# Block 1 of a two-block transformer kernel: the last down-projection on all 512 tokens at once

## The chip, the cores and the metric

The kernel runs on one core of a Trainium2 chip, as one program from the loading of the inputs to the storing of the result. The metric is the time of one execution in microseconds (us) on the device; of several runs the median counts. The engines are named as the profile names them: PE is TensorE (matrix products; PEld is its loading of weights, which runs beside them), DVE is VectorE, ACT is ScalarE, POOL is GpSimd, and SP is SyncE, which issues most of the loads.

## The reference

One sequence of 512 tokens of width 1024 passes through two blocks of two layers each, in float32. The part that the change touches is the second half of a layer of block 1:

```python
for l in range(DEPTH):                                   # DEPTH = 2
    ...                                                  # three mixers, added to x
    u = _rms_norm(x, mlp_norm_g[l]) @ w_up[l]            # 1024 -> 4096
    x = x + jnp.square(jax.nn.relu(u)) @ w_down[l]       # 4096 -> 1024

    gate = jax.nn.sigmoid((_rms_norm(x, ple_norm_g[l]) @ w_ple_gate[l]).astype(jnp.float32))
    e = _rms_norm(p[l] @ w_ple_proj[l], ple_post_norm_g[l]).astype(jnp.float32)
    x = x + (gate * e).astype(x.dtype)
```

Here `_rms_norm` divides each token by the root of its mean square and multiplies by a gain, and `p[l]` is a second input of width 256. Block 2 has attention mixers and a gated feed-forward part with a convolution, each behind a modulated norm, and a last norm.

## The kernel before, in words

**Layout.** `x` is held transposed: eight tiles `x[m]` of 128 features by 512 tokens. A product in float32 is made of three matrix products of rounded parts: `mm3` (line 171) issues, for each 128 rows of the contraction, high by high (L176), low weight or high weight by the other's low part (L177, L178), all into one bank of the accumulator memory. `split` (line 134) makes the parts: ACT casts to the high part (L136), DVE subtracts (L137). `feat_group` (line 181) makes `ng` output tiles of 128 features for the tokens of each slice in `parts`; a slice is all 512 tokens (`FULL`) or one of two halves of 256 (`HALVES`).

**Banks.** An output tile goes to a bank by rotation (`mm`, line 105). Inside `wide` and `held` the rotation is over three names: `ps_mm` with 3 buffers, `ps_S` with 2 and `ps_T` with 2. A group can begin when the reader of the bank's last content is done. The small products of the norms take `ps_mm` too.

**Norms.** `norm_stats` (line 244) works on one half of the tokens in three steps. First the squares of the eight tiles are made on ACT (L252, L255) and added on DVE (L256, into `n_acc`). Then PE sums over the features with four small matmuls of one column (L260); DVE scales the sums (L121); POOL makes the inverse root in ten small operations (L122 to L128); ACT writes it on the diagonal of `n_dg`, twice (L264). Last, PE spreads it over the partitions (L267) and ACT copies the result to a tile `R` (L268). Below, a *chain* is the way from L260 to L267 of one half. The steps are a generator: `start` runs the first and queues the rest, and `tick` takes the next step when enough matmul work has been issued (table `PAUSES`, line 29).

**The end of a layer of block 1** is `mlp1` (line 900). The 4096 hidden features come in 8 chunks: `up(c)` makes 512 of them, `down(c)` multiplies them by their part of `w_down` and adds them into `yacc` (L947, DVE). `down(7)` adds its product straight to `x` (L942, DVE). Behind it six chains run one after the other while PE does other products:

- #1 and #2, for the halves 0 and 1: the norm of `x` ahead of the gate (`pre`, the result in `g_R`); beside its squares `hsplit` makes the parts of `x` times gain (ACT L283, DVE L284) that the gate's product reads;
- #3 and #4: the norm of `p @ w_ple_proj` (`enorm`). The product has 16 groups (L992 to L995, ACT copies them to `yacc`). Behind the norm, DVE multiplies the eight tiles of the half by gain and norm (L984, eight times);
- #5 and #6: the norm for the next layer or block (`nxt`), started behind each half of the gate.

The gate has eight groups for each half (weights `w_pg1`). Its sink `gsink` (lines 986 to 991) multiplies by `g_R` straight out of the bank (L988, DVE), takes tanh (L989, ACT), multiplies with `yacc` (L990, DVE) and adds to `x` (L991, DVE). L990 needs the result of L984.

**Order.** The program text says what depends on what; the order of the instructions on each engine is set when the program is built, by a scheduler that sees the whole program. On the chip each engine then takes its instructions strictly in that order. So a small edit can move instructions far from its place.

Of the kernel before, what the change touches and what calls it, by code (L numbers as in the profile page):

```python
# [39 lines left out]
FULL = (slice(0, S),)  # L40
HALVES = (slice(0, S // 2), slice(S // 2, S))
# [20 lines left out]
class Builder:  # L62
# [837 lines left out]
    def mlp1(self, l, fp, act, nxt):  # L900
# [4 lines left out]
        acts = {}  # L905
# [33 lines left out]
        def down(c):  # L939
            def sink(m, pt, sl):  # L940
                if c == 7:
                    nc.vector.tensor_tensor(self.x[m][:, sl], self.x[m][:, sl], pt, ALU.add)  # L942
                    return
                if c == 0:
                    nc.scalar.copy(yacc[m], pt)
                else:
                    nc.vector.tensor_tensor(yacc[m], yacc[m], pt, ALU.add)  # L947
                if c == 6:
                    nc.vector.tensor_tensor(yacc[m], yacc[m], R2, ALU.mult)
                    nc.vector.tensor_tensor(self.x[m], self.x[m], yacc[m], ALU.add)  # L950
            ws = [self.wload("w_dn1", l * 16 + c * 2 + g, 4 * 512) for g in range(2)]
            for sl in HALVES if c == 7 else FULL:
                for g in range(2):
                    self.feat_group(ws[g], 4, 4, acts[c], sink, 4 * g, (sl,))
                if c == 7:
                    self.start(pre(sl))
        up(0)
        self.flush()
# [2 lines left out]
        for c in range(1, 8):  # L961
            up(c)
            self.mod_part(l, fp, (c - 1) * 6, c * 6)
            down(c - 1)
# [7 lines left out]
        self.mod_part(l, fp, 42, 48)  # L972
        self.mod_done(l, fp)
        down(7)

        act, ee = pre.st["act"], yacc
# [19 lines left out]
        ws = [self.wload("w_pg1", l * 4 + g, 8 * 256, (lambda: self.mtile(fp)) if g >= 2 else None) for g in range(4)]  # L996
# [574 lines left out]
```

## Time and profile before

| | |
|---|---|
| runs | 2770.52, 2776.11, 2781.68 us; median 2776.11 |
| profiled execution | 2770.02 us; span of the trace 2768.2 us; mean granted clock of TensorE 0.989 |
| PE busy | 2691.5 us (97% of the span), 16360 matmuls |
| DVE, ACT, POOL busy | 1782.7 (64%), 1182.1 (43%), 233.0 us (8%) |
| `down(7)` on PE | layer 0 from 625.42 us, layer 1 from 1327.50 us |
| DMA | 285.59 MB, mean 103 GB/s |

The times in the trace are from the start of the span. A matmul's own duration overlaps the next one's, so the pace of PE is read from the distance between starts. The number in brackets at the end of a row of the timeline is the time that the engine sat idle before this instruction, and what ended it.

### The profile page before, as it was taken

Reading aid. Unit: us, or ns where it says so; the run is one execution under the profiler, and the core shown is the slowest. Engines: PE = TensorE matmul, PEld = TensorE weight load, DVE = VectorE, ACT = ScalarE, POOL = GpSimd, SP = SyncE. Lnnn points to the kernel's source line nnn. Section 1 sums busy time; section 2 is a strip of 40 time slices with the busy share of each in tenths; the row PEclk is TensorE's granted clock in tenths of the full one; section 3 lists DMA queues with packets and bytes.
Section 4 is the critical chain, followed back from the end, with each engine's and each line's share of the span. In section 5 each row is a group of like instructions: output and inputs, shape, how many; then the busy total and the mean of one; then the engine's idle time right before and its main releaser. Section 6 shows DMA issues by size and latency. Waiting matters only on the chain.

```text
span 2768.2 us, 42721 instructions
## 1 busy us (share of the span) xinstructions
PE 2691.5 (97%) x16360; PEld 2287.3 (83%) x16360; DVE 1782.7 (64%) x3888; ACT 1182.1 (43%) x2340; POOL 233.0 (8%) x606
## 2 busy tenths in 40 slices
PE   8999999999999999999999999999999999999998
PEld 7876988889977788778988777888889787888887
DVE  7677777568767767765863676655554476664555
ACT  4644532326374543233543555333234455532332
POOL 2000100002200010000122300000001310000000
PEclk9999999999999999999999999999999999999999
DMA  4211487332321127843323211233332312133222
GB/s 155 77 40 54 143 266 229 111 103 92 92 73 47 55 89 238 254 156 100 107 67 110 62 57 63 84 88 101 99 94 80 118 37 78 51 103 99 88 86 78
DMA packets 87644, 285.59 MB, mean 103 GB/s; under 512 B 10972, under 2 KB 15132, under 8 KB 87440
## 3 DMA queue, kind: packets, MB, share of 16 engines
q1 hardware_dynamic: 81280, 266.49, 30.1%
q0 software_dynamic: 5872, 16.35, 2.3%
q8 instruction: 128, 2.10, 0.3%
q14 instruction: 76, 0.62, 0.1%
q10 hardware_dynamic: 288, 0.03, 0.0%
HBM read 280.69 MB, written 2.14 MB: 102 GB/s over the span
## 4 chain that ended last, share of the span: by engine, by line
PE 80%; DVE 8%; DMA 5%; ACT 3%; issue 2%; POOL 2%; SPq 0%; DVEq 0%; ACTq 0%; POOLq 0%
PE ps_mm L176 13%; PE ps_mm L177 12%; PE ps_mm L178 12%; PE ps_T L176 5%; PE ps_T L177 5%; PE ps_T L178 5%; PE ps_S L176 5%; PE ps_S L177 5%; PE ps_S L178 5%; DMA wm<-w_mod 4%; PE ps_S L1091 2%; PE ps_o L1137 1%; DVE wm L1034 1%; PE ps_T L1131 1%; PE ps_S L582 1%
## 5 line engine op out<-in xcount | busy, mean ns | idle before, releaser
L136 ACT CAST wh<-wr 128x1024 fp32r<-128x1024 f32 (+4 forms) x414 | 406.6, 986 | 659.4 <-PE ps_mm L177 209.4
L137 DVE TENSOR_TENSOR wl<-wr,wh 128x1024 fp32r<-128x1024 f32 (+4 forms) x414 | 474.8, 1148 | 306.7 <-ACT wh L136 300.2
L176 PE MATMUL ps_mm<-slotA,wh 128*128 128x512 f32 (+1 forms) x632 | 227.1, 365 | 1.8 <-ACT slotA L317 0.7
L177 PE MATMUL ps_mm<-slotA,wh 128*128 128x512 f32 (+1 forms) x632 | 225.7, 359 | 2.0 <-DVE slotA L318 2.0
L178 PE MATMUL ps_mm<-slotA,wl 128*128 128x512 f32 (+1 forms) x632 | 224.7, 357 | 0.0
L176 PE MATMUL ps_mm<-wh,slotA 128*128 128x256 f32 (+3 forms) x688 | 207.6, 303 | 1.1 <-ACT slotB L1084 1.1
L178 PE MATMUL ps_mm<-wh,slotA 128*128 128x256 f32 (+3 forms) x688 | 205.9, 299 | 0.0
L177 PE MATMUL ps_mm<-wl,slotA 128*128 128x256 f32 (+3 forms) x688 | 205.9, 300 | 0.0
L1034 DVE CUSTOM_DVE_ANT_0 wm<-wm,sc 128x1024 f32<-128x1024 f32 x96 | 117.5, 1224 | 67.6 <-DMA wm<-w_mod 66.7
L136 ACT CAST m_h<-tmp 128x512 fp32r<-128x512 f32 (+1 forms) x122 | 71.3, 587 | 208.1 <-DVE tmp L913 171.8
L176 PE MATMUL ps_mm<-slotB,wh 128*128 128x512 f32 (+1 forms) x408 | 143.8, 357 | 3.4 <-ACT slotB L136 2.6
L176 PEld LDWEIGHTS ps_mm<-wh,slotA 128*128 128x128 f32 x688 | 131.1, 191 | 14.3 <-issue 10.6
L177 PE MATMUL ps_mm<-slotB,wh 128*128 128x512 f32 (+1 forms) x408 | 141.9, 349 | 0.0
L178 PE MATMUL ps_mm<-slotB,wl 128*128 128x512 f32 (+1 forms) x408 | 140.9, 346 | 0.0
L176 PEld LDWEIGHTS ps_mm<-slotA,wh 128*128 128x128 f32 x632 | 120.5, 193 | 21.3 <-issue 3.2
L177 PEld LDWEIGHTS ps_mm<-wl,slotA 128*128 128x128 f32 x688 | 131.1, 191 | 7.9 <-issue 6.8
L177 PEld LDWEIGHTS ps_mm<-slotA,wh 128*128 128x128 f32 x632 | 120.7, 191 | 19.8 <-DVE slotA L318 2.9
L178 PEld LDWEIGHTS ps_mm<-slotA,wl 128*128 128x128 f32 x632 | 120.8, 191 | 19.3 <-issue 3.9
L178 PEld LDWEIGHTS ps_mm<-wh,slotA 128*128 128x128 f32 x688 | 131.3, 191 | 4.5 <-issue 3.2
L1107 ACT ACTIVATE at_s<-at_s,at_st 128x512 f32<-128x512 f32 (+3 forms) x160 | 89.4, 559 | 104.0 <-DVE at_st L1105 96.2
L176 PE MATMUL ps_S<-m_h,wh 128*128 128x512 f32 (+1 forms) x355 | 129.4, 365 | 0.7 <-DVE yacc L947 0.4
L178 PE MATMUL ps_S<-m_h,wl 128*128 128x512 f32 (+1 forms) x355 | 129.2, 364 | 0.0
(633 smaller groups left out, 7183.9 us busy)
## 6 DMA issues: line engine op xcount, KB each, us to landing
wr<-w_up SPq DMA_DIRECT2D x152, 512.0 KB, 3.9
wm<-w_mod SPq DMA_DIRECT2D x96, 512.0 KB, 4.6
wr<-w_dn SPq DMA_DIRECT2D x64, 512.0 KB, 3.9
wr<-w_dn SPq DMA_DIRECT2D x32, 384.0 KB, 3.1
wr<-w_dn SPq DMA_DIRECT2D x32, 320.0 KB, 2.8
wr<-w_f SPq DMA_DIRECT2D x16, 512.0 KB, 3.7
wr<-w_pg SPq DMA_DIRECT2D x16, 512.0 KB, 3.8
wr<-w_t SPq DMA_DIRECT2D x12, 512.0 KB, 4.7
```

Source lines behind the costliest of these rows:

```text
L136: nc.scalar.copy(hi, src)
L137: nc.vector.tensor_tensor(lo, src, hi.bitcast(F32), ALU.subtract)
L176: nc.tensor.matmul(out, ah, bh, start=i == 0, stop=False)
L177: nc.tensor.matmul(out, ah, bl, start=False, stop=False)
L178: m = nc.tensor.matmul(out, al, bh, start=False, stop=i == n - 1)
L582: nc.tensor.matmul(pt, qs[f][b:b + 64, tt], qs[4][b:b + 64, k0:k0 + w], start=True, stop=True)
L1034: nc.vector.tensor_tensor_reduce(w, w, self.sc, 1.0, 0.0, ALU.mult, ALU.add, accum_out=self.mod[l][:, j:j + 1])
L1091: i = nc.tensor.matmul(pts[u], q, k, start=True, stop=True, tile_position=None if row is None else (row, 0))
L1107: nc.scalar.activation(s, s, AF.Exp, bias=st[:, 0:1], scale=-1.0, accum_out=st[:, 1:2])
L1131: nc.tensor.transpose(tp[:, c * P:c * P + P], s[:, c * P:c * P + P], self.ident)
L1137: nc.tensor.matmul(po[u * 64:u * 64 + 64], v(c, u), pT[:, c * P:c * P + P], start=c == 0, stop=c == t, tile_position=(0, u * 64))
```

## The change

The two groups of `down(7)` (four output tiles each) are no longer made once for each half of the tokens, but once for all 512. The norms of both halves are started behind them. The weights, the sums and the results are the same; `down(0)` to `down(6)` are as they were. Both layers of block 1 are touched.

```diff
             ws = [self.wload("w_dn1", l * 16 + c * 2 + g, 4 * 512) for g in range(2)]
-            for sl in HALVES if c == 7 else FULL:
-                for g in range(2):
-                    self.feat_group(ws[g], 4, 4, acts[c], sink, 4 * g, (sl,))
-                if c == 7:
+            for g in range(2):
+                self.feat_group(ws[g], 4, 4, acts[c], sink, 4 * g)
+            if c == 7:
+                for sl in HALVES:
                     self.start(pre(sl))
```

In each layer 192 matmuls of 256 columns become 96 of 512, and 16 additions of 128x256 become 8 of 128x512. The groups of `down(7)` fall from 16 to 8, so that every later group gets another bank of the rotation. The new order of the instructions has these places.

DVE in `down(7)` of layer 0, difference of the two orders (L942 adds a product to `x`, L284 and L256 are of chain #1, L137 is the low part of weights):

```order
-L942 TENSOR_TENSOR x<-x,ps_T 128x256
-L942 TENSOR_TENSOR x<-x,ps_mm 128x256
+L942 TENSOR_TENSOR x<-x,ps_T 128x512
 L950 TENSOR_TENSOR x<-x,yacc 128x512
-L942 TENSOR_TENSOR x<-x,ps_S 128x256
 L284 SCALAR_TENSOR_TENSOR slotA<-x,vec_0_89,slotA 128x256
-L256 TENSOR_TENSOR n_acc<-tmp,n_acc 128x256
-L942 TENSOR_TENSOR x<-x,ps_T 128x256
+L942 TENSOR_TENSOR x<-x,ps_mm 128x512
 L284 SCALAR_TENSOR_TENSOR slotA<-x,vec_0_89,slotA 128x256
```

A full-width addition now frees both halves of a tile at once, and the parts and squares of both halves come mixed behind it.

PE in layer 0 at L267 of chain #4 (`ps_mm_...`, `ps_S_...` are banks with the number of the tile that is in them; `slotA` and `m_h` are the parts of `x` and of gate weights). First the order of before:

```order
L178 MATMUL ps_S_7035<-slotA_6036,m_l_6492 128x256
L267 MATMUL ps_mm_6824<-n_dg_6821,ones_83 128x256 [waits Activation_49]
L176 MATMUL ps_mm_6890<-slotA_6022,wh_6467 128x256
L177 MATMUL ps_mm_6890<-slotA_6023,wh_6467 128x256
L178 MATMUL ps_mm_6890<-slotA_6022,wl_6468 128x256
```

Then that of the change:

```order
L178 MATMUL ps_T_6923<-slotA_6036,m_l_6380 128x256
L267 MATMUL ps_mm_6712<-n_dg_6709,ones_83 128x256 [waits Activation_49]
L176 MATMUL ps_S_6983<-slotA_6022,m_h_6397 128x256 [waits DVE_49]
L177 MATMUL ps_S_6983<-slotA_6023,m_h_6397 128x256
L178 MATMUL ps_S_6983<-slotA_6022,m_l_6398 128x256
```

Behind L267 stood a group into a `ps_mm` bank that waits for nothing, and the next group into a `ps_S` bank whose last reader comes behind L984 began 50 matmuls later; now such a group follows at once, and it waits for DVE. DVE's order at the same place has the reader (L988 of `ps_S_6778`, whose bank `ps_S_6983` takes) behind the eight L984, which need this L267:

```order
L984 SCALAR_TENSOR_TENSOR yacc_3377<-yacc_3377,vec1_0_89,R1_85 128x256
L284 SCALAR_TENSOR_TENSOR slotB_6734<-x_72,vec1_1_91,slotB_6733 128x256
L284 SCALAR_TENSOR_TENSOR slotB_6736<-x_72,vec1_1_91,slotB_6735 128x256
L256 TENSOR_TENSOR n_acc_6755<-tmp_6763,n_acc_6755 128x256
L284 SCALAR_TENSOR_TENSOR slotB_6738<-x_72,vec1_1_91,slotB_6737 128x256
L256 TENSOR_TENSOR n_acc_6755<-tmp_6766,n_acc_6755 128x256
L256 TENSOR_TENSOR n_acc_6755<-tmp_6769,n_acc_6755 128x256
L988 TENSOR_TENSOR tmp_6803<-ps_S_6778,g_R_3378 128x256
```

In before, two L988, out of `ps_mm_6890` and `ps_S_6920`, stood right behind the last L984.

PE in layer 1 at L267 of chain #3, in the order of the change:

```order
L177 MATMUL ps_T_13495<-slotB_12766,wh_13088 128x256
L267 MATMUL ps_mm_13272<-n_dg_13219,ones_83 128x256 [waits Activation_49]
L260 MATMUL ps_mm_13358<-ones_83,n_acc_13063 128x1 [waits DVE_49]
L260 MATMUL ps_mm_13358<-ones_83,n_acc_13063 128x1
L176 MATMUL ps_mm_13385<-slotB_12755,m_h_13130 128x256 [waits DVE_49]
```

L260 of chain #4 follows L267 of chain #3 without a product between; in before 25 matmuls stood there. The matmuls between L260 and L267 of each chain, counted from the two orders:

| chain | #1 | #2 | #3 | #4 | #5 | #6 |
|---|---|---|---|---|---|---|
| layer 0 before | 67 | 72 | 70 | 72 | 70 | 48 |
| layer 0 changed | 60 | 63 | 62 | 73 | 64 | 69 |
| layer 1 before | 67 | 72 | 71 | 80 | 68 | 72 |
| layer 1 changed | 66 | 59 | 65 | 31 | 25 | 72 |

Two chains in the middle of the layers of block 2 change as well: from 24 to 64 matmuls in its first layer, and from 47 to 14 in its second.

## Rows read from the trace of the kernel before

**Rows 1.** The page: its head and the busy time of each engine.
```profile
span 2768.2 us, 42721 instructions
PE 2691.5 (97%) x16360; PEld 2287.3 (83%) x16360; DVE 1782.7 (64%) x3888; ACT 1182.1 (43%) x2340; POOL 233.0 (8%) x606
```

**Rows 2.** Timeline, PE around the start of down(7): start, duration, instruction.
```profile
617.26 0.39 PE L176 MATMUL ps_T<-m_h,wh 128*128 128x512 f32 x1
...
619.98 0.39 PE L176 MATMUL ps_mm<-m_h,wh 128*128 128x512 f32 x1
...
625.42 0.28 PE L176 MATMUL ps_T<-m_h,wh 128*128 128x256 f32 x1
...
626.85 0.28 PE L176 MATMUL ps_mm<-m_h,wh 128*128 128x256 f32 x1
```

**Rows 3.** Groups of DVE from 600 to 650 us: count, then busy us, mean ns.
```profile
L950 DVE TENSOR_TENSOR x<-x,yacc 128x512 f32<-128x512 f32 x8 | 5.5, 687 | 0.1
...
L942 DVE TENSOR_TENSOR x<-x,ps_T 128x256 f32<-128x256 f32 x5 | 2.1, 419 | 0.6 <-PE ps_T L178 0.6
```

**Rows 4.** Timeline, PE and ACT in layer 0: chains #4, #5 and #6.
```profile
695.36 0.59 PE L267 MATMUL ps_mm<-n_dg,ones 128*128 128x256 f32 x2
...
696.25 0.35 ACT L268 COPY R<-ps_mm 128x256 f32<-128x256 f32 x1
...
698.90 0.50 PE L260 MATMUL ps_mm<-ones,n_acc 128*128 128x1 f32 x4
...
701.98 0.28 PE L176 MATMUL ps_S<-slotA,m_h 128*128 128x256 f32 x1
...
709.91 0.70 PE L267 MATMUL ps_mm<-n_dg,ones 128*128 128x256 f32 x2 [2.01 <-ACT n_dg L264]
...
727.71 0.51 PE L260 MATMUL ps_mm<-ones,n_acc 128*128 128x1 f32 x4
...
734.93 0.70 PE L267 MATMUL ps_mm<-n_dg,ones 128*128 128x256 f32 x2 [0.86 <-ACT n_dg L264]
```

**Rows 5.** Timeline, DVE in layer 0 around L984 behind chain #4.
```profile
692.27 0.47 DVE L284 SCALAR_TENSOR_TENSOR slotB<-x,vec,slotB 128x256 fp32r<-128x256 f32 x1
692.67 0.94 DVE L256 TENSOR_TENSOR n_acc<-tmp,n_acc 128x256 f32<-128x256 f32 x2
...
697.86 3.25 DVE L984 SCALAR_TENSOR_TENSOR yacc<-yacc,vec,R 128x256 f32<-128x256 f32 x8
701.03 0.42 DVE L988 TENSOR_TENSOR tmp<-ps_mm,g_R 128x256 f32<-128x256 f32 x1
701.36 0.42 DVE L988 TENSOR_TENSOR tmp<-ps_S,g_R 128x256 f32<-128x256 f32 x1
```

**Rows 6.** Timeline, DVE in layer 1: neighbours whose starts give three prices.
```profile
1398.64 0.42 DVE L256 TENSOR_TENSOR n_acc<-tmp,n_acc 128x256 f32<-128x256 f32 x1
1398.98 0.42 DVE L988 TENSOR_TENSOR tmp<-ps_mm,g_R 128x256 f32<-128x256 f32 x1
...
1399.64 1.22 DVE L137 TENSOR_TENSOR wl<-wr,wh 128x1024 fp32r<-128x1024 f32 x1
1400.78 0.42 DVE L988 TENSOR_TENSOR tmp<-ps_T,g_R 128x256 f32<-128x256 f32 x1
```

**Rows 7.** Timeline, PE in layer 1: chains #4 and #5, and L260 of #6.
```profile
1382.34 0.50 PE L260 MATMUL ps_mm<-ones,n_acc 128*128 128x1 f32 x4
...
1392.38 0.59 PE L267 MATMUL ps_mm<-n_dg,ones 128*128 128x256 f32 x2
...
1409.70 0.70 PE L267 MATMUL ps_mm<-n_dg,ones 128*128 128x256 f32 x2
...
1425.86 0.71 PE L260 MATMUL ps_mm<-ones,n_acc 128*128 128x1 f32 x4 [4.73 <-DVE n_acc L256]
...
1427.00 0.41 PE L178 MATMUL ps_mm<-slotA,wl 128*128 128x256 f32 x1
...
1429.56 0.32 PE L178 MATMUL ps_mm<-slotA,wl 128*128 128x256 f32 x1
```

**Rows 8.** Busy us of the engines in a stretch; PEclk is the granted clock.
```profile
1420.00:1430.00 10.00, 5.27 (x32) 5.07 (x31) 6.14 (x23) 3.89 (x12) 3.83 (x14) 0.83 0.16 38
```

**Rows 9.** Timeline, block 2: a chain of its first and one of its second layer.
```profile
1736.10 0.70 PE L267 MATMUL ps_mm<-n_dg,ones 128*128 128x256 f32 x2 [1.85 <-ACT n_dg L264]
...
2398.01 0.51 PE L260 MATMUL ps_mm<-ones,n_acc 128*128 128x1 f32 x4
2402.55 0.70 ACT L264 ACTIVATE n_dg<-ident,rt 128x128 f32<-128x128 f32 x2 [3.67 <-POOL rt L128]
```

## The prediction

> **What bounds the kernel now.** I read the head of the page first: PE is busy for 2691.5 of 2768.2 us [rows 1]. It is the engine that sets the end, and only about 77 us are left in which it is not busy. So an edit can gain in two ways, fewer or cheaper matmuls or one of the few idle stretches gone, and it can lose by making PE wait where it does not wait now. The second view is the timeline of PE at `down(7)`. A group of 12 matmuls of 512 columns takes 2.72 us (617.26 to 619.98), one of 256 columns 1.43 (625.42 to 626.85): 0.227 and 0.119 us for each, so that two halves cost a little more than one whole [rows 2]. The third view is the timeline of the six norm chains behind it. There I looked for a bracket behind L267, which says that PE came to it before the chain was done. In layer 0 only #5 (2.01 us) and #6 (0.86) have one [rows 4]; in layer 1 no L267 of block 1's six has one, but L260 of #6 is preceded by 4.73 us in which PE waits for DVE's sums [rows 7]. So the chains are nearly covered by products, and with little to spare. A chain's own length shows where PE waited for it: 727.71 to 734.93 is 7.2 us, 698.90 to 709.91 is 11.0 [rows 4]. The least in the trace is in block 2, from 2398.01 to the end of L264 at 2403.25, 5.2 us [rows 9]. Cover is read as matmuls between L260 and L267 times 0.12 us, plus 0.4 for L260 itself: 80 matmuls give 10.0, and the trace has 1382.34 to 1392.38 [rows 7].
>
> **The change, part by part.** All sums are against the profiled execution of 2770.0 us, which lies 6.1 below the median of the three runs, 2776.1.
>
> *Removed work.* In each layer 192 x 0.1195 = 22.95 us of matmuls become 96 x 0.2267 = 21.76: 1.2 us less, 2.4 in all, straight off PE. DVE's additions fall from 32 of 0.42 us to 16 of 0.69 [rows 3], 2.4 us less over both layers. That is worth nothing by itself, as PE is the cover; with PE waiting for DVE it would shorten a wait by at most that.
>
> [...]
>
> *Moved work.* The first half of `x` was complete after half of `down(7)`, and chain #1 then ran beside the second half. Now both halves are complete at its end: relative to the products behind it, chain #1 starts some 96 matmuls later, 11 us. The chains must run one after the other (one `n_dg`, one `R`), so that the series starts late and has to catch up. The table of matmuls between L260 and L267 shows where the order catches up: chains #1 to #3 lose 1 to 13 matmuls each, and in layer 1 #4 is left with 31 and #5 with 25. POOL's ten operations for each chain keep their order, and no wait is added there. On SP a few loads of weights change places; no product in these stretches waited for a weight, and I cost that at nothing, because the same loads stand ahead of the same groups.
>
> *Chain #2.* Covered by 63 matmuls in layer 0 (8.0 us) and 59 in layer 1 (7.5). The length with an idle DVE is 7.2. But L121 now stands behind casts and sums: in layer 1 two L137 of 1.14 us [rows 6] are right ahead of it. With 1.2 and 1.6 us for that the waits are **0.4 and 1.3 us**. Bounds: nothing (length 5.2), and 3.0 and 3.5 (11.0). I take values near 7.2, since this is the same stage.
>
> *Layer 0, behind chain #4.* 73 matmuls (9.2 us) cover it. But right behind L267 stands a group into a `ps_S` bank. Its last reader is an L988 that DVE reaches only after the eight L984, which need this L267. In before that place held a `ps_mm` group, and a `ps_S` group with such a reader came 50 matmuls later, at 701.98, when L988 (701.36 + 0.42) had just left the bank [rows 4, 5]: no more than 0.2 us to spare. Now the cover is gone. From L267 to that L988 it was 6.0 us; six operations, three L284 (0.40) and three L256 (0.34), now stand where one L988 (0.33) stood [rows 5, 6], 1.9 more. 7.9 and 0.4 for L988 make 8.3 from L267, less 0.2 for L267 itself: 8.1 us. That is the upper bound; the lower is 6.9, since 1.2 of it was DVE still busy (R was there at 696.60, L984 began at 697.86). I take **7.5**. What is queued behind: L260 of #5 and everything that follows on PE.
>
> [...]
>
> [...]
>
> *Layer 0, #5 and #6.* #5 now starts after the wait, on a quieter DVE, with 64 matmuls (8.1) and #6 has 69 (8.7) in place of 48, against a length of 7.2. Both brackets go: **-2.0 and -0.9**. Layer 0: -1.2 + 0.4 + 7.5 + 1.4 - 2.9 = **+5.2**.
>
> *Layer 1.* #4: 31 matmuls cover 4.1 us of a chain of 5.2 to 7.2: between 1.1 and 3.1, I take **2.5**, nearer the length in this stage. Then a `ps_T` group waits as in layer 0, but 96 matmuls (11.5 us, and 0.6 for the two L260 and L267) after L267. DVE needs, from L267, about 3.2 until it is through with its backlog (2.5 in layer 0 [rows 4, 5], and the two halves' L984 now follow closer), 3.5 for L984 and one L990, eleven short operations of 0.34, three L137 of 1.14 and L988: 14.2 us. **2.1**; bounds 0 and 3. #5: 25 matmuls cover 3.4 us; 7.2 less 3.4 is 3.8, and L121 stands behind fourteen short operations, of which little sticks out: **4.0**, bounds 1.8 and 7.6. From there on DVE sets the pace: L267 of #5 to L260 of #6 took 16.2 us with PE idle 4.73 at its end [rows 7], the same operations stand there now, so what is late at L267 is late at L260. [...] Layer 1: -1.2 + 1.3 + 2.5 + 2.1 + 4.0 = **+8.7**.
>
> *Block 2.* The wait of 1.85 [rows 9] goes, as 64 matmuls cover it. In the other layer 14 matmuls (2.1 us) stand against 5.2: 3.1 new. **+1.2**; bounds -2 and +3.
>
> Sum: 5.2 + 8.7 + 1.2 = 15.1. 2770.0 becomes 2785.1, and on the median of the runs 2776.1 becomes **2791 us**, 0.54% slower. A measurement of this kernel tells about 0.5%, 14 us, from no change; the forecast lies at that edge.
>
> **Rivals.**
> *1. The norms stay covered: not slower.* Place: L267 of #4 and #5 in layer 1, and the `ps_S` bank in layer 0. If DVE, ACT and POOL, which wait beside PE, ran the chains in less than the cover, only the savings would be left: 2.4 of matmuls and the brackets of 2.0, 0.9 and 1.85, 7.2 us, 2769. It decides at a chain of 3.4 us or less. Against it: no chain in the trace is under 5.2. For it: these lengths are read from stretches in which DVE was busy, and in layer 1 of before no L267 waited. Chance 0.10, with 0.03 beyond 0.5% faster.
> *2. The late start is given back in the tail of layer 1.* While PE waits in layer 1, DVE can go on with sinks and casts that stand later now. If they fill the waits, the 16.2 us after #5 shrink, by no more than the 4.73 that PE idled there and the 1.4 of clock: 6.1 less, 2785. For it: that stretch is full of DVE work. Against it: DVE's order is fixed, and the work is behind the late chain. Chance 0.25.
> *3. The catching up costs more.* Each of the four chains of layer 1 and layer 0 that are now tight runs nearer to 11.0 than to 7.2, 1.5 us more each: 6 more, 2797. It needs DVE's queue ahead of L121 to be as full as at 698.90. For it: the squares of both halves and the casts now come in one crowd. Chance 0.20.
>
> **How the numbers follow.** The forecast has 0.45, with a range of its own of 2786 to 2796; 0.28 of it is over the 0.5% (2790), 0.17 under. Slower by over 0.5%: 0.28 + 0.20 = 0.48. Within: 0.17 + 0.25 + 0.07 = 0.49. Faster: 0.03. The range takes in rivals 2 and 3 with 3 us around them and part of rival 1: 2775 to 2800.
>
> **What would show it.** Right: in `down(7)` 96 matmuls 0.227 apart; in layer 0 an idle PE of 7 to 8 us ahead of a `ps_S` group right behind L267 of #4, put down to DVE, with a granted clock below 1 behind it, and no bracket at #5 and #6; in layer 1 brackets of 2 to 3 us at #4 and about 4 at #5; in block 2 one bracket gone and one of 3 us new. Wrong: no wait at that `ps_S` group, a chain under 5 us from L260 to L267, or L260 of #6 in layer 1 less than 5 us later than 1425.86. What would fell the whole argument is a PE busy time that falls by far more than 2.4 us.

## The result, and the profile after

The changed kernel takes 2805.5 us (median of four runs, 2801.8 to 2808.4) against 2775.6 before: 1.0113 times as long, interval 1.0091 to 1.0136 (the two medians by themselves give 1.0108). The forecast was 2791 with a range of 2775 to 2800; the result lies above it. The direction was right; the loss is 30 us, twice the 15.1 that the sum gave.

From here "later" is counted so: at which time has PE issued the same number of matmul columns (elements of the moving operand) in both traces? That gives the lateness at any point, also where instructions changed places.

| stage, in the time of before | forecast | measured |
|---|---|---|
| to 610 us | 0 | +0.6 |
| 610 to 745: norm series of layer 0 | +5.2 | +9.4 |
| 745 to 1327: the rest of layer 0, the mixers and most of the feed-forward part of layer 1 | 0 | +1.8 |
| 1327 to 1440: norm series of layer 1 | +8.7 | +12.6 |
| 1440 to 1760: first layer of block 2 | -1.9 | +2.5 |
| 1760 to the end | +3.1 | +4.8 |

(The -1.9 is the bracket of 1.85 that the prediction let go; the 3.1 its new wait in block 2.) A stage is good to a few us: in this and the eight kernels below in which the first stage holds the same work in the same order, it read between +0.6 and +7.8. That it is above zero in all nine says that the profiled execution of before, 2770.0 us against a median of 2775.6, was a quick one. The figures of the two series are the firmest, as the lateness hardly moves just ahead of them and just behind.

The page of the changed kernel, its head and the groups of one bank:
```profile
span 2800.0 us, 42301 instructions
...
PE 2695.8 (96%) x16168; PEld 2285.7 (82%) x16168; DVE 1783.0 (64%) x3872; ACT 1182.0 (42%) x2340; POOL 228.6 (8%) x606
...
L176 PE MATMUL ps_S<-m_h,wh 128*128 128x512 f32 (+1 forms) x325 | 122.4, 376 | 6.4 <-DVE yacc L947 6.4
```
PE has 192 matmuls fewer than in [rows 1], and yet 4.3 us more busy time: it ran part of them at a lower granted clock (mean of the span 0.984, in before 0.989). The span is 31.8 us longer, so 27.5 us of it are idle. Of PE's idle time in front of L267 alone, 20.5 us stand here and 8.0 in before. The last line is a wait of a kind that the prediction did not have (below).

Timeline of the changed kernel, PE in layer 0: `down(7)`, then chains #2 to #5.
```profile
625.98 0.39 PE L176 MATMUL ps_T<-m_h,wh 128*128 128x512 f32 x1
...
628.70 0.39 PE L176 MATMUL ps_mm<-m_h,wh 128*128 128x512 f32 x1
...
663.68 0.61 PE L260 MATMUL ps_mm<-ones,n_acc 128*128 128x1 f32 x4 [1.24 <-ACT g_R L268]
...
689.53 0.51 PE L260 MATMUL ps_mm<-ones,n_acc 128*128 128x1 f32 x4
...
703.10 0.70 PE L267 MATMUL ps_mm<-n_dg,ones 128*128 128x256 f32 x2 [4.21 <-ACT n_dg L264]
...
710.31 0.58 PE L176 MATMUL ps_S<-slotA,m_h 128*128 128x256 f32 x1 [6.51 <-DVE tmp L988]
...
722.80 0.59 PE L267 MATMUL ps_mm<-n_dg,ones 128*128 128x256 f32 x2
```
A group of `down(7)` takes 2.72 us, as the whole groups of [rows 2]: the saving of 1.2 us for each layer is there. The wait at the `ps_S` group right behind L267 of chain #4 is there too, 6.51 us. But in front of it stands one of 4.21 us that the sum had at nothing: chain #4 took 13.6 us, from 689.53 to 703.10. The bracket at #5 is gone.

The same stretch on DVE:
```profile
691.41 0.14 DVE L121 TENSOR_SCALAR n_v<-ps_mm 128x2 f32<-128x2 f32 x1
...
695.47 0.48 DVE L284 SCALAR_TENSOR_TENSOR slotB<-x,vec,slotB 128x256 fp32r<-128x256 f32 x1
695.87 1.21 DVE L137 TENSOR_TENSOR wl<-wr,wh 128x1024 fp32r<-128x1024 f32 x1
...
700.15 0.42 DVE L256 TENSOR_TENSOR n_acc<-tmp,n_acc 128x256 f32<-128x256 f32 x1
...
704.35 3.25 DVE L984 SCALAR_TENSOR_TENSOR yacc<-yacc,vec,R 128x256 f32<-128x256 f32 x8
...
709.84 0.42 DVE L988 TENSOR_TENSOR tmp<-ps_S,g_R 128x256 f32<-128x256 f32 x1
```
and on POOL:
```profile
691.72 0.22 POOL L122 TENSOR_SCALAR g_rt<-n_v 128x2 int32<-128x2 int32 x1 [11.50 <-ACT tmp L989]
...
695.68 4.94 POOL L126 TENSOR_TENSOR n_t<-n_t,n_v 128x2 f32<-128x2 f32 x1
...
702.13 0.19 POOL L128 TENSOR_TENSOR g_rt<-n_t,g_rt 128x2 f32<-128x2 f32 x1
```
POOL's part of the chain, from L122 to the last L128, took 10.6 us. It is thirteen operations (L122 and three rounds of L125 to L128), not ten as the description of the kernel and the prediction have it. One L126 of two elements a partition, 0.19 us at the median, took 4.94. It ended at 700.62, when DVE's unbroken row of operations ended (700.15 + 0.42 = 700.57). From L267 to the L988 that frees the bank it is 6.7 us (703.10 to 709.84); from 704.35 on DVE did the eight L984, three L284, three L256 and this L988 in the order that was set for it.

Such a long POOL operation is not new with the change. POOL and DVE in the kernel before, in chain #5 of layer 0, whose 11.0 us the prediction read:
```profile
702.26 3.11 POOL L122 TENSOR_SCALAR rt<-n_v 128x2 int32<-128x2 int32 x1 [8.31 <-DVE n_v L121]
...
704.23 1.09 DVE L991 TENSOR_TENSOR x<-x,yacc 128x256 f32<-128x256 f32 x3
```
Here L122 took 3.11 us and ended at 705.37, DVE's row at 705.32. In the thirteen traces with the root on POOL (before, the change, and all runs below but e5 and e6), 21 of 5250 POOL operations of 128x2 took 2.0 us or more. Each ended 0.05 to 0.08 us after a DVE operation, and each stood beside a row of DVE that holds L990 or L991, the last two steps of the gate's sink.

Timeline of the changed kernel, PE in layer 1: L267 of chain #2, L267 of #4 with two matmuls behind it, the first group that waits for L988, L267 of #5, L260 of #6.
```profile
1386.39 0.70 PE L267 MATMUL ps_mm<-n_dg,ones 128*128 128x256 f32 x2 [0.81 <-ACT n_dg L264]
...
1407.68 1.22 PE L267 MATMUL ps_mm<-n_dg,ones 128*128 128x256 f32 x2 [4.90 <-ACT n_dg L264]
...
1409.13 0.42 PE L178 MATMUL ps_mm<-slotB,wl 128*128 128x256 f32 x1
1409.34 0.41 PE L176 MATMUL ps_mm<-slotB,wh 128*128 128x256 f32 x1
...
1424.19 0.39 PE L176 MATMUL ps_T<-slotB,m_h 128*128 128x256 f32 x1 [1.59 <-DVE tmp L988]
...
1433.25 0.70 PE L267 MATMUL ps_mm<-n_dg,ones 128*128 128x256 f32 x2 [2.60 <-ACT n_dg L264]
...
1449.41 1.01 PE L260 MATMUL ps_mm<-ones,n_acc 128*128 128x1 f32 x4 [4.73 <-DVE n_acc L256]
```
Stretches of the changed kernel, columns as in [rows 8]: the wait of layer 0 and what follows it, then those of layer 1.
```profile
700.00:710.00 10.00, 0.70 (x2) 0.30 (x2) 6.67 (x18) 4.19 (x12) 1.82 (x7) 0.69 0.18 57
710.00:720.00 10.00, 9.69 (x67) 9.69 (x68) 5.52 (x15) 3.96 (x10) 3.46 (x15) 0.80 0.01 2
...
1400.00:1410.00 10.00, 5.10 (x33) 4.72 (x32) 8.63 (x23) 3.34 (x8) 6.00 (x12) 0.85 0.16 52
1410.00:1420.00 10.00, 10.00 (x71) 10.00 (x71) 7.73 (x17) 3.70 (x7) 0.00 (x0) 0.81 0.17 54
...
1450.00:1460.00 10.00, 10.00 (x66) 10.00 (x67) 0.76 (x7) 1.54 (x5) 2.58 (x13) 0.76 0.01 1
```
The four forecast waits of layer 1 were 1.3, 2.5, 2.1 and 4.0; they are 0.81, 4.90, 1.59 and 2.60. Each is off; that their sum is 9.9 both times is luck. The tail is as forecast: from L267 of #5 to L260 of #6 16.16 us, in before 16.16 [rows 7]. Not in the sum was the clock behind the 4.90: the granted clock is 0.85 and 0.81, the matmuls there start 0.21 us apart (1409.13 to 1409.34), and from 1408 to 1413 us it is 0.50. In the two stretches 104 matmuls took 15.1 us of busy time; at the 0.119 of [rows 2] that would be 127, so some 2.7 us. The clock fell behind the 2.60 too (granted 0.83 from 1430 to 1440), which made the lateness 1.5 us larger at 1438; by 1444 that was given back, as PE waits for DVE there in either kernel. Behind the 4.73 us at L260 of #6, as long as in before, the matmuls stay 0.213 us apart until 1454.7, for 5.3 us, where before had it for 3.7 (1425.86 to 1429.56): 0.9 us more. The same count for 710 to 720 gives 67 against 81, 1.7 us, where the sum had 1.4. Behind both waits, from 710 to 714 us and from 1449.41 to 1454, the granted clock is 0.50.

In block 2 the bracket of 1.85 in [rows 9] is gone, as forecast. Two other waits stand ahead of its place, and the wait in the other layer is there, 2.86 against 3.1. Timeline of the changed kernel, PE in block 2:
```profile
1735.40 0.87 PE L1147 MATMUL ps_T<-ident,tmp 128*128 128x128 f32 x3 [2.46 <-DVE tmp L1145]
...
1737.81 1.01 PE L176 MATMUL ps_mm<-slotB,wh 128*128 128x256 f32 x3 [1.53 <-ACT slotB L136]
...
2434.12 1.02 PE L267 MATMUL ps_mm<-n_dg,ones 128*128 128x256 f32 x2 [2.86 <-ACT n_dg L264]
```

### The profile page after: what moved, and what is told of

It is laid out like the page before. It is cut to its first block, busy times and chain, and to the rows that moved or that the text cites. A ratio compares the mean times of both kernels' runs of the same rounds, so it can differ in the third digit from the quotient of the medians.

```text
span 2800.0 us, 42301 instructions
## 1 busy us (share of the span) xinstructions
PE 2695.8 (96%) x16168; PEld 2285.7 (82%) x16168; DVE 1783.0 (64%) x3872; ACT 1182.0 (42%) x2340; POOL 228.6 (8%) x606
## 3 DMA queue, kind: packets, MB, share of 16 engines
q8 instruction: 127, 2.08, 0.3%
## 4 chain that ended last, share of the span: by engine, by line
PE 79%; DVE 8%; DMA 6%; ACT 3%; issue 2%; POOL 2%; SPq 0%; DVEq 0%; ACTq 0%; POOLq 0%
PE ps_mm L176 12%; PE ps_mm L177 12%; PE ps_mm L178 12%; PE ps_T L176 5%; PE ps_T L177 5%; PE ps_T L178 5%; PE ps_S L176 5%; PE ps_S L177 5%; PE ps_S L178 5%; DMA wm<-w_mod 5%; PE ps_S L1091 2%; PE ps_o L1137 1%; DVE wm L1034 1%; PE ps_T L1131 1%; DVE wl L137 1%
## 5 line engine op out<-in xcount | busy, mean ns | idle before, releaser
L137 DVE TENSOR_TENSOR wl<-wr,wh 128x1024 fp32r<-128x1024 f32 (+4 forms) x414 | 474.4, 1147 | 312.8 <-ACT wh L136 304.9
L176 PE MATMUL ps_mm<-slotA,wh 128*128 128x512 f32 (+1 forms) x668 | 243.4, 369 | 1.9 <-ACT slotA L317 1.1
L177 PE MATMUL ps_mm<-slotA,wh 128*128 128x512 f32 (+1 forms) x668 | 241.6, 363 | 1.5 <-DVE slotA L318 1.4
L178 PE MATMUL ps_mm<-slotA,wl 128*128 128x512 f32 (+1 forms) x668 | 240.4, 362 | 0.0
L176 PEld LDWEIGHTS ps_mm<-slotA,wh 128*128 128x128 f32 x668 | 128.1, 194 | 23.6 <-issue 3.2
L178 PEld LDWEIGHTS ps_mm<-slotA,wl 128*128 128x128 f32 x668 | 128.3, 192 | 21.5 <-issue 3.9
L177 PEld LDWEIGHTS ps_mm<-slotA,wh 128*128 128x128 f32 x668 | 128.4, 192 | 20.7 <-issue 2.2
L176 PEld LDWEIGHTS ps_mm<-wh,slotA 128*128 128x128 f32 x688 | 130.6, 190 | 14.2 <-issue 10.6
L176 PE MATMUL ps_S<-m_h,wh 128*128 128x512 f32 (+1 forms) x325 | 122.4, 376 | 6.4 <-DVE yacc L947 6.4
L178 PE MATMUL ps_S<-m_h,wl 128*128 128x512 f32 (+1 forms) x325 | 122.2, 376 | 0.0
```

The lines of the kernel that those rows point to most:

```text
L137: nc.vector.tensor_tensor(lo, src, hi.bitcast(F32), ALU.subtract)
L176: nc.tensor.matmul(out, ah, bh, start=i == 0, stop=False)
L177: nc.tensor.matmul(out, ah, bl, start=False, stop=False)
L178: m = nc.tensor.matmul(out, al, bh, start=False, stop=i == n - 1)
```

## The experiments

The edit holds two things. The norm series starts late (called W in the expectations). And eight groups fewer in each layer shift the rotation of the banks for all that follows (called B): the three names repeat every three groups, eight fewer is a shift by one for each layer. `self.nmm` counts the groups, so adding to it sets the rotation without adding work. With another rotation the scheduler also makes another order: of the 3888 DVE operations, 131 stand in another place in e4 than in before, though the work is the same. So "the rotation" means below the banks and the order that comes with them; no run parts the two. All of these kernels compute the whole reference; the three probes at the end add a stretch of their own. In the table the stages are those of the first table, us later than before in one profiled execution each; the ratio is that of the timed runs.

| run | to 610 | series 0 | to 1327 | series 1 | to 1760 | to the end | ratio, interval |
|---|---|---|---|---|---|---|---|
| the change | +0.6 | +9.4 | +1.8 | +12.6 | +2.5 | +4.8 | 1.0113, 1.0091 to 1.0136 |
| e1 | +6.0 | +10.0 | -0.6 | +5.8 | +1.6 | +0.8 | 1.0081, 1.0061 to 1.0101 |
| e2 | +5.7 | 0.0 | -2.8 | +8.0 | +0.5 | -0.7 | 1.0030, 1.0017 to 1.0044 |
| e3 | +3.8 | +6.8 | -3.5 | +5.3 | -1.4 | +1.8 | 1.0035, 1.0022 to 1.0048 |
| e4 | +1.9 | -1.3 | +4.0 | +4.3 | +3.3 | +7.2 | 1.0037, 1.0022 to 1.0053 |
| e5 | +12.6 | +8.4 | -0.8 | +7.3 | -2.0 | +5.4 | 1.0094, 1.0077 to 1.0111 |
| e6 | +14.2 | +6.2 | -0.8 | +11.5 | -2.9 | +4.2 | 1.0087, 1.0072 to 1.0102 |
| e7 | +1.7 | +2.9 | -0.1 | +3.8 | -0.1 | -0.1 | 1.0015, 1.0006 to 1.0025 |
| e8 | +7.7 | -2.2 | -3.1 | +1.7 | 0.0 | +2.5 | 0.9987, 0.9978 to 0.9996 |
| e9 | +7.8 | +0.2 | +4.6 | +2.0 | +0.8 | +5.3 | 1.0032, 1.0017 to 1.0047 |
| e10 | +3.0 | -1.3 | +0.5 | +2.6 | +1.5 | -1.3 | 1.0013, 1.0004 to 1.0022 |

The profiled executions of e4, e8 and e9 lie 3.8, 6.0 and 9.2 us above the medians of their runs, so their stages sum to more than their ratios say.

**e1 and e2: one layer at a time.** The loop of before stays for the other layer.
```diff
-            for sl in HALVES if c == 7 else FULL:
+            halved = c == 7 and l == 1
+            for sl in HALVES if halved else FULL:
                 for g in range(2):
                     self.feat_group(ws[g], 4, 4, acts[c], sink, 4 * g, (sl,))
-                if c == 7:
+                if halved:
+                    self.start(pre(sl))
+            if c == 7 and not halved:
+                for sl in HALVES:
                     self.start(pre(sl))
```
(e2 has `l == 0`.)

> The full-width last down-projection in layer 0 of block 1 alone; layer 1 keeps its halves. Theory W (the norm series starts late and is squeezed; the loss lies in the series behind each full-width product): the trace shows the +9 us of the changed kernel behind down(7) of layer 0 and no more than 3 us behind that of layer 1, in all +10 to +14 us. Theory B (the loss comes from the banks that the later groups get, which move by one place in the rotation): about half of the 30 us, spread over layer 0, layer 1 and block 2. Rival L (the loss is nearly all in layer 1): under +5 us.

> The full-width last down-projection in layer 1 alone. Layer 0 should read as in the kernel before. Theory W: +9 to +13 us behind down(7) of layer 1, with an idle PE at L267 of chain #4 or #5. Theory B: loss behind layer 1 and in block 2 about equal, 5 us each. If the two single-layer kernels add up to much less than the 30 us of both, the rest is in what both together do to the rotation.

e1 lost 0.81%, 20 to 22 us, more than the 10 to 14 expected; e2 lost 6 to 8 us, less than the least of 9 that W gave. The two ratios add up to the whole, 0.81 and 0.30 against 1.13. Layer 0 alone costs 10.0 us in its own series, about as in the change. But e1 also loses 5.8 us in the series of layer 1, where W allowed 3 and whose code is untouched: there only the rotation has shifted. So the time that a layer loses does not all come from that layer's own edit, and B does something. In e2 the sign that W named is not there: no L267 of #4 or #5 in layer 1 waits. PE in layer 1 of e2, and the stretch behind the wait (lines past the edit are four higher, so that L992 is L988):
```profile
1411.06 0.58 PE L176 MATMUL ps_S<-slotB,m_h 128*128 128x256 f32 x1 [4.55 <-DVE tmp L992]
...
1410.00:1420.00 10.00, 8.94 (x52) 8.94 (x53) 6.48 (x20) 2.48 (x6) 2.06 (x11) 0.66 0.15 41
```
This is the wait at the `ps_S` group that the change has in layer 0. Both of these series run with the rotation shifted by one place; in layer 1 of the change it is shifted by two.

**e3 and e4: the two halves of the edit apart.** e3 is the change with the banks put back; e4 is before with the banks of the change.
```diff
# e3, on the change
             if c == 7:
+                self.nmm += 2
                 for sl in HALVES:
# e4, on before
+            if c == 7:
+                self.nmm += 1
```

> Both layers full-width, but the rotation of the banks is moved on by two places behind down(7), so that every later group gets the bank name that it has in the kernel before. Theory W: still slower, +15 to +22 us, all of it behind down(7) of the two layers; block 2 as before (0 to 1 us). Theory B: the loss is gone, between -3 and +4 us.

> The kernel before, with halves, but with the rotation moved on by one place behind down(7), so that every later group gets the bank name that it has in the changed kernel. Theory W: little behind down(7) (0 to +4 us in each layer), and the 6 us of block 2 and 2 us of layer 1's feed-forward part that the changed kernel lost: +6 to +12 us in all. Theory B: +20 to +30 us.

e3 lost 8 us and e4 11. Neither theory has the total of e3: it is above what B gave and half of what W gave; that of e4 is what W gave. The stages part them. In e3 the two series lose 6.8 and 5.3 us, by the waits forecast, smaller. Timeline of e3, PE, at #4 and #5 of each layer (lines past the edit are one higher):
```profile
702.36 0.70 PE L267 MATMUL ps_mm<-n_dg,ones 128*128 128x256 f32 x2 [1.59 <-ACT n_dg L264]
...
710.69 0.39 PE L176 MATMUL ps_S<-slotA,m_h 128*128 128x256 f32 x1 [3.34 <-DVE tmp L989]
...
1412.50 0.39 PE L176 MATMUL ps_S<-slotB,m_h 128*128 128x256 f32 x1 [1.44 <-DVE tmp L989]
...
1420.82 0.70 PE L267 MATMUL ps_mm<-n_dg,ones 128*128 128x256 f32 x2 [1.87 <-ACT n_dg L264]
```
The granted clock of the stretches 700 to 710 and 710 to 720 us is 1.00 and 0.97 in e3, where the change has 0.69 and 0.80: the shorter waits cost next to no clock there. In e4 the series of layer 0 loses nothing (-1.3); it loses in layer 1 and in block 2, behind the shift. Timeline of e4, PE in block 2:
```profile
1720.58 0.87 PE L1149 MATMUL ps_T<-ident,tmp 128*128 128x128 f32 x3 [2.65 <-DVE tmp L1147]
...
1722.99 1.01 PE L176 MATMUL ps_mm<-slotB,wh 128*128 128x256 f32 x3 [1.53 <-ACT slotB L136]
...
2420.70 1.22 PE L267 MATMUL ps_mm<-n_dg,ones 128*128 128x256 f32 x2 [2.86 <-ACT n_dg L264]
```
These are the change's three waits in block 2, in a kernel that has the halves of before: the rotation makes them. The bracket of 1.85 is gone in e4 too, while e3 keeps it and lacks the 2.86. So both theories hold a part. Their sum, 8 and 11, is short of 30 by some 11 us (1.13 less 0.35 and 0.37 is 0.41%; by the three intervals, good to some 8 us). The series of layer 0 has 3.9 us of it (9.4 against 6.8 and -1.3), that of layer 1 3.0 (12.6 against 5.3 and 4.3); the rest is not placed.

The table shows how the two fail to add up: what the late series costs hangs on the rotation that it runs in. In the series of layer 1 the whole width costs 5.3 us more than the halves with the banks of before (e3 against before), 2.2 with a shift by one (e2 8.0, e1 5.8) and 8.3 with a shift by two (the change 12.6, e4 4.3), each from one execution.

**e5 and e6: the root on DVE.** If POOL's operations make the chain long, DVE, which needs ten for the same root, should do them faster. One default argument is changed, on before (e5) and on e3 (e6).
```diff
-    def norm_stats(self, xs, sl, R, rt, gp=True):
+    def norm_stats(self, xs, sl, R, rt, gp=False):
```

> Control for the next one: the kernel before, with the inverse root of every norm on DVE (ten operations of two columns) and none on POOL. Theory P (the length of a chain is made on POOL, whose small operations are held up while DVE is full): chains from L260 to L267 of 3 to 4 us where PE waits for them, the brackets of 2.0, 0.9 and 1.85 us gone, -3 to -8 us in all. Rival D (what counts is DVE's queue, and it becomes longer by the ten operations): -1 to +5 us.

> Full-width in both layers, banks as in the kernel before (the kernel that was 8 us slower, +12 us behind the two products), and the inverse root on DVE as in the control. Theory P: the +12 us behind the two products fall to +4 or less, and the whole is within 3 us of the control. Rival D (a late series that must give back its delay, waits of banks behind L984, whatever the chain's length): it stays 6 to 10 us slower than the control.

The opposite came: 0.94% slower on before, that is 26 us where 3 to 8 were to be gained. Timeline of e5, DVE in chain #4 of layer 0, three of its operations:
```profile
705.35 0.15 DVE L130 TENSOR_TENSOR n_t<-g_rt 128x2 f32<-128x2 f32 x1
705.75 1.22 DVE L137 TENSOR_TENSOR wl<-wr,wh 128x1024 fp32r<-128x1024 f32 x1
...
708.29 0.15 DVE L131 TENSOR_TENSOR n_t<-n_t,n_v 128x2 f32<-128x2 f32 x1
```
L131 depends on L130, which takes 0.15 us, and yet it starts 2.9 us after it: in DVE's order operations of other products stand between the steps of the chain, such as the L137 of 1.22 us. That chain took 15.7 us from L260 (700.12) to L267 (715.81), and PE waits 24.1 us in front of L267 in all, against 8.0 before. It begins with the first norm of the program, whose L267 waits 4.59 us against 0.38: 4.2 of the 12.6 us in the first stage. e6 stays within 3 us of e5 as the expectation for it said, but for another reason: its control had lost as much already. Both theories missed e5, and so their test by e6 fails. In these two kernels POOL's queue is the better place; the runs say nothing on how much POOL itself is held.

**e7: half the lateness.** Only the second half of `down(7)`'s output tiles is done in halves, with the banks as before.
```diff
+            self.feat_group(ws[0], 4, 4, acts[c], sink, 0)
             for sl in HALVES if c == 7 else FULL:
-                for g in range(2):
-                    self.feat_group(ws[g], 4, 4, acts[c], sink, 4 * g, (sl,))
+                self.feat_group(ws[1], 4, 4, acts[c], sink, 4, (sl,))
                 if c == 7:
                     self.start(pre(sl))
+            if c == 7:
+                self.nmm += 1
```

> Half the dose: the first four output tiles of the last down-projection full-width, the other four in halves, with the banks as in the kernel before. The first norm starts about 5 us later than before, instead of 11. Theory W (the lateness of the series is what costs): about half of the 12 us behind the two products, +4 to +7 us there. Rival S (only a certain lateness costs, the waits come from a chance meeting of groups and banks): 0 to +2 us, or 10 and more.

The series lose 2.9 and 3.8 us, 6.7 together where e3 lost 12.1: half the lateness, about half the loss, as W has it. The time is 0.15% up, e3's 0.35%. New in layer 0 of its trace are 0.88 us at the `ps_S` group and 0.55 at L267 of #4; the 2.08 at L267 of #5 was there in before (2.01).

**e8: the change with something in front.** If the lateness costs, then a chain that is ready earlier should fill it. `down(7)` is moved behind the first half of the projection whose norm (`enorm`) is one of the six chains, so that this chain runs beside it; the 512-token form and its saving stay, banks as before.
```diff
             if c == 7:
+                self.nmm += 2
...
-        down(7)
-
-        act, ee = pre.st["act"], yacc
+        ee = yacc
...
         for sl in HALVES:
             self.feat_group(w, 2, 8, pe, lambda m, pt, sl: nc.scalar.copy(ee[m][:, sl], pt), 0, (sl,))
             self.start(enorm(sl))
+            if not sl.start:
+                down(7)
+        act = pre.st["act"]
```

> Full-width in both layers, banks as before, and one norm is taken out of the crowd: the projection of the first half's second input and its norm are put ahead of the last down-projection, so that its chain runs beside these matmuls and only five follow. Theory W: the loss behind the two products goes to between -3 and +3 us, and the kernel is about as fast as before. Rival D: the waits at the banks stay, +5 us or more.

Measured 2770.8 against 2774.1, ratio 0.9987 (0.9978 to 0.9996): both series lose nothing together (-2.2 and +1.7), and the kernel is a little faster than before. Timeline of e8, PE: the two L267 of layer 1's series with a bracket, L260 of #6, and the wait of block 2, which is that of before.
```profile
1377.77 0.70 PE L267 MATMUL ps_mm<-n_dg,ones 128*128 128x256 f32 x2 [1.35 <-ACT n_dg L264]
...
1413.78 0.70 PE L267 MATMUL ps_mm<-n_dg,ones 128*128 128x256 f32 x2 [1.05 <-ACT n_dg L264]
...
1430.08 0.64 PE L260 MATMUL ps_mm<-ones,n_acc 128*128 128x1 f32 x4 [4.73 <-DVE n_acc L256]
...
1740.30 0.70 PE L267 MATMUL ps_mm<-n_dg,ones 128*128 128x256 f32 x2 [1.85 <-ACT n_dg L264]
```

**e9 and e10: the same kernel in the two other rotations.** e8 without its `self.nmm += 2` (the banks of the change), and with `self.nmm += 1`.

> The last kernel (projection of the first half ahead of the full-width product) without the move of the rotation, so that later groups get the bank names of the changed kernel. Theory I (the rotation costs by itself, outside the norm series: in layer 1's feed-forward part and in block 2, as with the halves and shifted banks): +6 to +9 us there and less than 5 us behind the two products. Rival J (the rotation costs mainly where it meets a squeezed series): within 3 us of the kernel before.

> The same with the third possible rotation. Theory I: block 2 has neither the long nor the short cover of the changed kernel, so 0 to +5 us in all. It also tells how far a result of one rotation can be taken as the value of the edit: a spread of 5 us and more between the three says that it can't.

The three rotations give 0.9987, 1.0032 and 1.0013: 0.45% or 9.9 us between the best and the worst, each against the kernel before as timed with it. The work is the same and the two series together lose little in all three (+0.2 and +2.0 in e9, -1.3 and +2.6 in e10), so with a chain ahead the late series costs next to nothing whatever the rotation. The order is not quite the same: 143 and 156 DVE operations of e8 stand elsewhere in e9 and e10. The spread is twice the 5 us above which, by the expectation of e10, one rotation's time can't be taken as the value of the edit. What e9 adds lies in layer 1's feed-forward part and in block 2, where theory I has it, 4.6 and 6.1 us in the one traced execution. In block 2 the three kernels with a shift of two there, the change, e4 and e9, lose 7.3, 10.5 and 6.1 us; all others between -0.2 and +3.4. The two waits at L1147 and behind it, 2.46 and 1.53 us in the change, are in all three, and in neither before nor e8; the same goes for the 2.86.

**e11 to e13: what holds POOL.** Before, with a stretch added behind its last output: POOL does 24 small `tensor_tensor` of 128x2 in a chain while DVE does a row of one kind, in outline:
```python
for i in range(24):
    nc.gpsimd.tensor_tensor(t, t, v, ALU.mult)
for i in range(36):
    nc.vector.tensor_tensor(outs[i % 4], a, b, ALU.add)
```
e11 has rows with two operands from the on-chip memory at 128x256, with one from a bank, with one tensor and a constant, and at 128x1024. In e12 no operation of DVE waits for another. e13 has in-place additions, operations with a constant or with one scalar for each partition, and a mixture.

> The kernel before with an added stretch behind the last layer, which measures a small POOL operation (128x2, two inputs) by itself: 12 with DVE idle, then 24 each beside DVE operations of 128x256 with two inputs from the state buffer, with one input from a bank, with one input, and of 128x1024 with two inputs. Theory H (POOL is held while DVE runs an unbroken row of operations with two inputs from the state buffer): 0.2 us alone, and one to several us beside the second and the last kind, with the first such operation ending when DVE's row ends. Rival: 0.2 to 0.4 us in all five, then the 4.94 us of the changed kernel have another cause.

> The probe again, but every DVE operation of a row writes a place of its own, so that none waits for an earlier one, as in the norm series of the kernel. 24 operations of 128x256 in each of the first three rows, six of 128x1024 in the last. Theory H (POOL gets in only where DVE's row of two-input operations is broken): one POOL operation of 5 to 8 us beside the row with two inputs from the state buffer and one of 5 to 7 us beside the wide row, each ending with DVE's row; 0.2 us beside the row with an input from a bank. Rival G (POOL waits for one DVE operation at most): no POOL operation over 1.3 us, as in the probe with waits.

> The probe a third time, with the kinds of DVE operation that stood beside the 4.94 us: a row of additions in place (as L256 and L991), one of three-operand operations with a constant (as L990), one with a scalar per partition (as L284), and a mixture of these with two of 128x1024 (as L137). POOL as before, 24 operations of 128x2 in each. Theory H' (a three-operand operation leaves POOL no gap to the next): in the second to fourth row one POOL operation of 4 to 8 us that ends with DVE's row. Rival G (no kind of DVE operation holds POOL for more than itself): none over 1.3 us, and the cause of the long POOL operations of the changed kernel stays open.

Timeline of e11, POOL: alone (12 operations), then 24 beside each row; the row of 8.71 us is beside one tensor and a constant, the last beside 128x1024.
```profile
2778.44 3.20 POOL L1405 TENSOR_TENSOR pb_t<-pb_t,pb_v 128x2 f32<-128x2 f32 x12
...
2782.43 7.97 POOL L1405 TENSOR_TENSOR pb_t<-pb_t,pb_v 128x2 f32<-128x2 f32 x24
...
2794.65 6.48 POOL L1405 TENSOR_TENSOR pb_t<-pb_t,pb_v 128x2 f32<-128x2 f32 x24
...
2807.15 8.71 POOL L1405 TENSOR_TENSOR pb_t<-pb_t,pb_v 128x2 f32<-128x2 f32 x24
...
2817.44 15.96 POOL L1405 TENSOR_TENSOR pb_t<-pb_t,pb_v 128x2 f32<-128x2 f32 x24
```
Alone an operation and the step to the next take 0.27 us (3.20 / 12). Beside DVE's additions of two 128x256 tensors from the on-chip memory they take 0.33, beside additions with one operand from a bank 0.27, as alone, and beside those of one tensor and a constant 0.36. Beside 128x1024 the row of 15.96 us holds two kinds: about half of the 24 ran while DVE did its row and took some 1.06 us each, one for each DVE operation (they start 1.14 us apart); the others ran behind it at 0.27. So POOL is held by such a DVE operation, for about one at a time. The instructions of L126 in the change, and of the probe line in e11 (count, then shortest, median and longest in ns):
```profile
L126 POOL TENSOR_TENSOR n_t<-n_t,n_v x75: 194/195/4941, 20.9 to 2778.2; 128x2 f32<-128x2 f32 x75
```
```profile
L1405 POOL TENSOR_TENSOR pb_t<-pb_t,pb_v x108: 194/195/1059, 2778.4 to 2833.2; 128x2 f32<-128x2 f32 x108
```
The longest in a probe's chain is 1.06 us, in e11 and e13 alike, and the first operation beside the wide row of e11 and e12, ahead of the chain, took 1.23: one DVE operation of 128x1024. No row, with the kernel's kinds of operation in it, made a wait over many of them as the 4.94 us in the change do. So the theories of the three expectations fell, as no operation lasted over several of DVE's, and e11's rival, 0.2 to 0.4 us beside every row, fell with the 1.06. What held is the rival of e12 and e13: POOL waits for one DVE operation at most, 1.23 us in the probes. The long wait in the change is no accident of one execution: e1, whose order on DVE is the same up to there, has it in the same chain. POOL in e1:
```profile
701.19 4.94 POOL L126 TENSOR_TENSOR n_t<-n_t,n_v 128x2 f32<-128x2 f32 x1
```
In the probes PE and ACT are idle, and none was made with them at work. Nor did a probe have L990 as the kernel has it, which writes over one of its own inputs and stood beside the long waits. What such a wait takes beyond one DVE operation stays open.

## Why the prediction was half right

Right were:
- *The mechanism.* A series of chains that starts later by half a `down(7)` makes PE wait where it did not. e3, e7 and e8 show it: with the banks held, 12.1 us lost in the two series, 6.7 with half the lateness, none when another chain is put ahead. The saving is real as well; e8 keeps it.
- *The `ps_S` bank in layer 0*: 6.51 us, where the sum had 7.5. From L267 to L988 it took 6.7 where 7.9 were counted. No run shows the 1.4 us of clock that stand in the sum of layer 0 and in rival 2; what the change showed in their place is a granted clock of 0.50 from 710 to 714 us and a loss of about 1.7.
- *The brackets of #5 and #6* in layer 0 are gone; the tail of layer 1 is unchanged; block 2 loses 1.85 and gains 2.86, though by the rotation and not by the late series (e4). That the waits of layer 1 sum to 9.9 as forecast is luck: each of the four was off by 0.5 to 2.4 us.
- *Rival 1*, covered norms: no. *Rival 2*, given back in the tail: no, 16.16 us both times. *Rival 3*, that catching up costs more because DVE's queue is full, is nearest to what came. It named the place, but gave it 6 us, and it had nothing outside the series.

Wrong were three steps.
1. *"73 matmuls (9.2 us) cover it"* (chain #4 of layer 0). The chain took 13.6 us and left 4.21. I took the length of a chain on a quiet DVE, 7.2, for a place where the edit had just put more on DVE, though 11.0 stood in the same rows [rows 4]. But 11.0 would have left only 1.8 to wait. The larger error is the sentence that POOL's operations "keep their order, and no wait is added there": the chain's 10.6 us on POOL hold one operation of 4.94 us. That term was put at nothing from the order alone, although the 11.0 of before held an operation of 3.11 us of the same kind. #4 in layer 1 was too short as well, 4.90 against 2.5. The 1.24 at L260 of #3, behind ACT's copy of the R of #2, belongs to chain #2 and was 0.4 in the sum. With 1.24, 4.21, 6.51, a clock loss of 1.7, less 2.9 for the two brackets and 1.2 saved, layer 0 comes to 9.6; measured is 9.4.
2. *The clock* was counted behind one wait. In layer 1 it costs some 2.7 us behind the 4.90 (granted 0.85 and 0.81 from 1400 to 1420). That and the waits, less the saving, make 11.4 of the 12.6 us; 0.9 more is the clock behind the 4.73 at L260 of #6, which stayed low for 5.3 us where before had 3.7.
3. *Nothing elsewhere.* The rotation of the banks was looked at only inside the two series and at two chains in block 2. It goes on behind them: in layer 1's feed-forward part a `ps_S` group waits for L947 twice, 3.2 us each time (the 6.4 of the page's group above), though before loses 4.3 in waits of its own in that stretch; in block 2 two waits of 2.46 and 1.53 come in the place of the 1.85. e4 shows what the rotation costs alone, 0.37%, e9 against e8 0.45%. Forecast for block 2 was +1.2, measured +7.3.

By the runs, the late series less the saving costs 8 us alone (e3) and the rotation 11 alone (e4); together they make 30. Of the other 11, good to some 8, the traces put 3.9 us in the series of layer 0 and 3.0 in that of layer 1, where the waits of the change are longer than those of e3 and fall with a low granted clock (0.69 and 0.80 from 700 to 720 us, 0.85 and 0.81 from 1400 to 1420); the rest is not placed. So the two parts are shown, and that they don't add up is shown; what lengthens the waits is not. POOL's 4.94 us is part of it by its place, in the chain that was 4.21 us late. In e3, with the same work and other banks, the longest POOL operations of that chain are 3.48 and 1.76 us (L127 and L128), and L267 is 1.59 late. The order on DVE differs between the two as well (169 of 3872 operations stand elsewhere, from 652 us on). That the order of DVE's row decides it would fit, but no run here shows the cause.

## What to carry to other kernels

A cheaper form of a product can cost far more than it saves when a serial chain waits for its first half: count the work between the chain's start and its end, and set it against the longest chain length seen under load, not the one on a quiet engine, with room to spare: the longest seen in before was 11.0 us, and here one took 13.6. An edit that changes the number of groups also turns every later rotation of buffers, and here the price of the edit itself hung on the rotation: hold it (here by one line) when the edit is tested, then try the other rotations by themselves. To keep the cheaper form, put another chain that is ready ahead of it (e8), whose gain of 0.13% is, however, smaller than what a rotation is worth.

## What was not expected of the hardware

- A POOL operation of 128x2, 0.19 us at the median, took 4.94 us beside an unbroken row of DVE operations and ended with that row; one of 3.11 us stood in the kernel before. In the probes the longest beside DVE was 1.23, one DVE operation of 128x1024.
- The rotation of the accumulator banks, with the order that the scheduler makes for it, moved the same work by 9.9 us, 0.45% of the time (e8 against e9).
- Ten small operations that depend on each other were slower on the engine that does each in 0.15 us (DVE: 15.7 us for the chain, the kernel 0.94% longer) than the thirteen of POOL, 0.27 us each when alone, as the faster engine's queue held other work between them.
